# Rotary embedding and attention scores: TensorE's steps as a loop, its waits relayed by GpSimd, and the small rests of five loads moved to one queue

## The chip, the cores and the metric

The kernel runs on one core of one Trainium2 chip. The metric is the device time of one execution in microseconds (us). Lower is better. The runs of the kernel before took 791.87, 792.61 and 793.0 us; their median is 792.61.

## What is computed

```python
# q, k: (16, 512, 16, 64) float32 as batch, sequence, heads, dim; cos, sin: (512, 32)
q1, q2 = q[..., :32], q[..., 32:]
q_rot = concat(q1 * cos - q2 * sin, q1 * sin + q2 * cos)   # k_rot from k in the same way
scores = einsum('bshd,bthd->bsht', q_rot, k_rot)            # (16, 512, 16, 512) float32
```

The output has 268.4 MB and the two inputs have 67.1 MB, so for each 4 MB of scores that go out, 1 MB of inputs comes in.

## The kernel before

A sequence of 512 rows is cut into 4 slots of 128 rows (row 4p+c lies in partition p of slot c). One **step** `i` makes the scores of one slot of queries against all 512 keys of its batch `i // 4`: 16 heads in 8 pairs `p`, 64 steps in all. Steps 0 to 3 are batch 0; there the work is cut by heads, so that it can begin before the whole batch is loaded.

In `scores` (L194 to L217) each pair is two matmuls of 64 rows by 512 columns into one of three PSUM tiles `ps`; ScalarE (ACT) copies the tile to a staging buffer `st` of 4 MB (L212); after pair 7 SyncE (SP) issues the store of the whole buffer (L192). There are three such buffers, so step `i` can begin its copies when the store of step `i-3` has landed.

Beside that, each step prepares a later slot of q and one of k. `rope` (L128 to L163) is three VectorE (DVE) instructions on 1024 elements for each slot: the product with the sines goes to `part` (L153), the product with the cosines stays in place (L154), and so does the sum (L158). `transposed` (L165 to L189) turns four blocks of 128x128 by TensorE (PE) into a PSUM `bank`, and a copy takes them to `qT` or `kT` (L189), by DVE for q and by ACT for k. q is turned one step ahead, k four steps ahead; both `qT` and `kT` have two buffers. In steps from 4 on q is turned after pairs 1 and 3, k after pairs 5 and 6 (L269 to L297). The order of the instructions on each engine is the order of the code (`manual_schedule`, L227); the waits between engines are put in by the framework. Each engine waits for the others' semaphores itself.

`load` (L117 to L126) brings 2 MB of q or k, one batch, at the end of every second step of four: q after step 4m+2, k after step 4m+3. SP issues them in line with the stores. Five of them, named in `RELIEVED` (L77), go another way, `load_around` (L89 to L114): GpSimd (POOL) issues 120 of the 128 partitions as one DMA. The trace's packets show it on 15 of the 16 DMA engines, and one and the same engine is left out each time. The code chooses that engine by a cursor that it moves round the DMA engines: `move_cursor` (L82 to L87) pushes it on by a tiny DMA on `n` partitions. The last 8 partitions, the rest, are 64 pieces of 2 KB. For two of the loads (k of batches 7 and 12) POOL issues them, and their packets are on eight DMA engines, those that the code counts as 8 to 15; for the three others (q of batches 6, 11 and 15) ACT issues them, and their packets are on the other eight, 0 to 7.

Of the kernel before, what the change touches and what calls it, by code (L numbers as in the profile page):

```python
# [7 lines left out]

@with_exitstack  # L10
def kernel(
# [19 lines left out]
    G = H // C  # L31

    const_pool = ctx.enter_context(tc.tile_pool(name="const", bufs=1))
    in_pool = ctx.enter_context(tc.tile_pool(name="in", bufs=2))
    part_pool = ctx.enter_context(tc.tile_pool(name="part", bufs=1))
    kt_pool = ctx.enter_context(tc.tile_pool(name="kt", bufs=2))
    qt_pool = ctx.enter_context(tc.tile_pool(name="qt", bufs=2))
    stage_pool = ctx.enter_context(tc.tile_pool(name="stage", bufs=3))
    ps_s_pool = ctx.enter_context(tc.psum_pool(name="ps_s", bufs=3))
    ps_t_pool = ctx.enter_context(tc.psum_pool(name="ps_t", bufs=2))  # L40

# [11 lines left out]
    ss_v = ss_t.rearrange("p c x j -> p c (x j)")  # L53

    st_first = [stage_pool.tile([P, H, S], fp32, tag="stage", name="st") for _ in range(2)]
    early = stage_pool.tile([P, 2 * C * H * D], fp32, tag="stage", name="early")
    units = {}
    used = [0]  # L60

    def load_units(which, head, heads, queues):
        n = C * heads * D
        t = early[:, used[0] : used[0] + n].rearrange("p (c e) -> p c e", c=C)
        used[0] += n
        src = dram[which][0, :, :, head : head + heads, :]
        dst = t.rearrange("p c (h d) -> p c h d", d=D)
        m = C // len(queues)
        for x, queue in enumerate(queues):
            queue.dma_start(dst[:, m * x : m * (x + 1)], src[:, m * x : m * (x + 1)])  # L70
        for h in range(0, heads, G):
            units[which, (head + h) // G] = t[:, :, D * h : D * (h + G)]

    batches = {}

# [3 lines left out]
    scratch = const_pool.tile([P, 96], fp32, name="scratch")  # L79
    tiny = [0]  # L80

    def move_cursor(n):  # L82

        y = tiny[0]
        tiny[0] += 1
        src = bass.AP(q.tensor, 512 * y, [(512, n), (64, 2), (1, 2)])
        nc.gpsimd.dma_start(scratch[:n, 4 * y : 4 * y + 4].rearrange("p (a b) -> p a b", a=2), src)  # L87

    def load_around(which, b, t):  # L89

        n, E, SMALL = 120, C * H * D, C * H * D // 8
# [3 lines left out]
        def pieces(queue, lo, hi, F):  # L97
            k = E // F
            src = bass.AP(d.tensor, d.offset + lo * E + E - F, [(E, hi - lo), (-F, k), (1, F)])
            v = t[lo:hi].rearrange("p c e -> p (c e)")  # L100
            dst = bass.AP(v.tensor, v.offset + E - F, [v.ap[0], (-F, k), (1, F)])
            queue.dma_start(dst, src)  # L102

        if x == 0:
            nc.gpsimd.inc_swdge_sem([], [], mode="reset_dge_cursor")
        else:

            move_cursor(16 - SLOW)
        if x % 2:
            move_cursor(8)  # L110
            pieces(nc.gpsimd, n, P, SMALL)
        move_cursor(SLOW + 1)
        pieces(nc.gpsimd, 0, n, E // 2)
        if not x % 2:  # L114
            pieces(nc.scalar, n, P, SMALL)

    def load(which, b):  # L117

        if b >= B:
            return  # L120
        t = in_pool.tile([P, C, H * D], fp32, tag=which + "_in", name=which + "_sb")
        batches[which, b] = t
        if (which, b) in RELIEVED:
            load_around(which, b, t)
        else:
            nc.sync.dma_start(t.rearrange("p c (h d) -> p c h d", h=H), dram[which][b])  # L126

    def rope(which, n):  # L128

        part = part_pool.tile([P, H * D], fp32, tag="part", name="part")
        if n < C:
            x = units[which, n]
            sv, k1, k2 = "p c (g j) -> p c g j", {"j": HD}, {"j": D}
            cs = cos_t.unsqueeze(2).to_broadcast((P, C, 2 * G, HD))
            ss = ss_v.unsqueeze(2).to_broadcast((P, C, G, D))
            pv = part.rearrange("p (c g j) -> p c g j", c=C, j=D)
            x5 = x.rearrange("p c (h x j) -> p c h x j", x=2, j=HD)
            p5 = part.rearrange("p (c h x j) -> p c h x j", c=C, x=2, j=HD)
            adds = [(x5[:, :, :, y], p5[:, :, :, 1 - y]) for y in range(2)]  # L140
        else:
            x = batches[which, n // C][:, n % C]
            sv, k1, k2 = "p (g j) -> p g j", {"j": HD}, {"j": D}
            cs = cos_t[:, n % C].unsqueeze(1).to_broadcast((P, 2 * H, HD))
            ss = ss_v[:, n % C].unsqueeze(1).to_broadcast((P, H, D))
            pv = part.rearrange(sv, **k2)
            x4 = x.rearrange("p (h x j) -> p h x j", x=2, j=HD)
            swapped = bass.AP(part.tensor, part.offset + HD, [part.ap[0], (D, H), (-HD, 2), (1, HD)])
            adds = [(x4, swapped)]
        xs, xc = x.rearrange(sv, **k2), x.rearrange(sv, **k1)  # L150

        def products():
            nc.vector.tensor_tensor(pv, xs, ss, op=mult)  # L153
            nc.vector.tensor_tensor(xc, xc, cs, op=mult)  # L154

        def sums():
            for y, z in adds:
                nc.vector.tensor_tensor(y, y, z, op=add)  # L158
# [3 lines left out]
    kT = {}  # L162
    qT = {}  # L163

    def transposed(which, n, g, copy):  # L165

        bank = ps_t_pool.tile([P, 4, P], fp32, tag="ps_t", name="bank")
        for x in range(4):
            if n < C:  # L170
                src = units[which, n][:, x, P * g : P * (g + 1)]
            else:
                src = batches[which, n // C][:, n % C, P * (4 * g + x) : P * (4 * g + x + 1)]
            nc.tensor.transpose(bank[:, x, :], src, ident)  # L174
        src = bank
        if which == "q":
            if n not in qT:
                qT[n] = qt_pool.tile([P, HP, P], fp32, tag="qT", name="qT_t")
            dst = qT[n][:, 4 * g : 4 * g + 4, :]
        else:  # L180
            b = n // C
            if b not in kT:
                kT[b] = kt_pool.tile([P, HP, S], fp32, tag="kT", name="kT_t")
            if n < C:
                dst = kT[b][:, 2 * n + g].rearrange("p (t c) -> p t c", c=C)
                src = bank.rearrange("p c t -> p t c")
            else:
                dst = kT[b][:, 4 * g : 4 * g + 4, P * (n % C) : P * (n % C + 1)]
        copy(out=dst, in_=src)  # L189

    def store(i, st):
        nc.sync.dma_start(o_v[i // C, i % C], st)  # L192

    def scores(i, p, st):  # L194

        ps = ps_s_pool.tile([P, 2, S], fp32, tag="ps_s", name="ps")
        b = i // C
        if b == 0:
            c, hp = divmod(p, 2)
            lhs, rhs = qT[i][:, C * hp + c], kT[0][:, 2 * i + hp]  # L200
        else:
            lhs, rhs = qT[i][:, p], kT[b][:, p]
        for r in range(2):
            po, rh = ps[:, r, :], rhs[64 * r : 64 * r + 64, :]
            nc.tensor.matmul(  # L205
                out=po, lhsT=lhs[64 * r : 64 * r + 64, :], rhs=rh, start=True, stop=True
            )
# [4 lines left out]
        nc.scalar.copy(out=so, in_=si)  # L212
        if b == 0 and p % 2 == 1:
            c = p // 2
            nc.sync.dma_start(o_v[0, c, :, G * i : G * (i + 1)], st[:, G * c : G * (c + 1)])
        elif b > 0 and p == HP - 1:
            store(i, st)  # L217

    def tr_act(which, n):
        for g in range(2):  # L220
            transposed(which, n, g, nc.scalar.copy)
# [5 lines left out]
    with tc.manual_schedule():  # L227
        nc.scalar.dma_start(sin_t, sin.rearrange("(p c) j -> p c j", c=C))
        load_units("k", 0, G, (nc.sync, nc.scalar))
        nc.sync.dma_start(cos_t, cos.rearrange("(p c) j -> p c j", c=C))  # L230
        load_units("q", 0, G, (nc.sync, nc.scalar))
        load_units("k", G, H - G, (nc.sync,))
        load_units("q", G, H - G, (nc.sync,))
        load("k", 1)
        load("q", 1)
        make_identity(nc, ident)
        nc.scalar.copy(out=ss_t[:, :, 0, :], in_=sin_t)
        nc.scalar.mul(ss_t[:, :, 1, :], sin_t, -1.0)
        for which in ("k", "q"):
            run(rope(which, 0))  # L240
            tr_act(which, 0)

        for i in range(C):
            st = st_first[i] if i < 2 else stage_pool.tile([P, H, S], fp32, tag="stage", name="st")
            if i < C - 1:
                dve = rope("k", i + 1) + rope("q", i + 1) + rope("k", C + i)
                nxt = [("k", i + 1), ("q", i + 1)]
            else:
                dve = rope("q", C) + rope("k", C + i) + rope("q", C + 1) + rope("k", 2 * C)  # L250
                nxt = [("q", C), ("k", C + i)]
            for p in range(HP):
                scores(i, p, st)
# [72 lines left out]
```

## Time and profile before

| What | us |
|---|---|
| Median of three runs (791.87 to 793.0) | 792.61 |
| Span of the profiled execution, first to last instruction | 789.9 |
| The median of the runs stands above that span by | 2.7 |
| End of the last DMA packet, in the span | 788.6 |
| PE busy (matmuls), DVE busy, ACT busy | 687.7, 543.8, 561.2 |
| Mean duration of one copy of a pair by ACT (L212, 512 of them) | 1.020 |
| Mean duration of one rope instruction by DVE (L153, L154, L158) | 1.22 |
| Store of 4 MB, median from issue to landing | 25.2 |

The span is the profiled execution's time without what lies around it (the launch and the end of the program); the page gives no other time of that execution. The view of busy time tells how long each engine worked, not whether anybody waited for it. That is told by the view of waits and by the slices of DMA: there a digit is the share of time, in tenths, in which the 16 DMA engines had a packet in work. Packets are the pieces that a DMA engine moves; the trace holds each one's queue, start, duration and size.

### The profile page before, as it was taken

The page shows a single profiled execution, that of the slowest core. Times are in us where ns is not written, and L with a number is a line of the kernel's source. Part 1 is how long each engine was busy: PE and PEld are TensorE (multiplying, and loading weights), DVE is VectorE, ACT ScalarE, POOL GpSimd, SP SyncE. Part 2 cuts the span into 40 slices and gives each one's busy share as a digit, 9 for nine tenths or more (in the row PEclk, how much of TensorE's full clock was granted, in tenths as well). Part 3 has the DMA queues.
Part 4 walks back from the last instruction along what each step waited for, and adds up shares of the span by engine and source line. Part 5 has one row for each costly group of instructions (what it writes and reads, how often), then busy time and mean ns, then how long its engine had stood idle before and what let it go on. Part 6 is the DMA issues. An engine that isn't in the chain of part 4 may idle for free.

```text
span 789.9 us, 7753 instructions
## 1 busy us (share of the span) xinstructions
PE 687.7 (87%) x3072; PEld 297.4 (38%) x3072; DVE 543.8 (69%) x516; ACT 561.2 (71%) x647; POOL 11.9 (2%) x24
## 2 busy tenths in 40 slices
PE   4999998989978989798897988989899798899960
PEld 2444443433423434243343433434334343344420
DVE  7999987667855859566676666767678486587400
ACT  3888886866847868486685865877577586588770
POOL 0000000000001000000000000100000000000000
PEclk9999999999998999899899898999899899899995
DMA  9999999999999999999999999999999999999997
GB/s 353 421 426 440 429 431 435 424 434 440 428 427 429 429 425 406 428 431 436 430 431 434 427 431 427 429 432 429 427 437 422 437 433 433 428 431 436 430 431 339
DMA packets 19100, 336.18 MB, mean 426 GB/s; under 512 B 2376, under 2 KB 3656, under 8 KB 4936
## 3 DMA queue, kind: packets, MB, share of 16 engines
q1 hardware_dynamic: 16288, 324.61, 96.1%
q0 software_dynamic: 1872, 10.10, 3.1%
q10 hardware_dynamic: 904, 0.98, 0.4%
q8 instruction: 24, 0.39, 0.2%
q14 instruction: 12, 0.10, 0.0%
HBM read 67.24 MB, written 268.44 MB: 425 GB/s over the span
## 4 chain that ended last, share of the span: by engine, by line
DMA 46%; PE 39%; DVE 7%; ACT 4%; issue 1%; ACTq 0%
DMA out_dram<-st 45%; PE ps L205 29%; PE bank L174 9%; ACT st L212 4%; DVE part L153 2%; DVE early L154 1%; DVE early L158 1%; DMA early<-in_q_dram 1%; DVE k_sb L158 1%; DVE k_sb L154 1%; DVE kT_t L189 0%; DVE q_sb L154 0%; DVE q_sb L158 0%; ACTq L321 0%; DVE qT_t L189 0%
## 5 line engine op out<-in xcount | busy, mean ns | idle before, releaser
L212 ACT COPY st<-ps 128x1024 f32<-128x1024 f32 x512 | 495.0, 1020 | 193.7 <-DMA out_dram<-st 109.1
L205 PE MATMUL ps<-kT_t,qT_t 64*128 64x512 f32 x2048 | 545.6, 650 | 64.3 <-ACT st L212 64.1
L205 PEld LDWEIGHTS ps<-kT_t,qT_t 64*128 64x128 f32 x2048 | 183.3, 196 | 255.3 <-issue 135.4
L189 DVE COPY qT_t<-bank 128x512 f32<-128x512 f32 x118 | 81.5, 690 | 186.5 <-PE bank L174 186.5
L174 PEld LDWEIGHTS bank<-ident,q_sb 128*128 128x128 f32 x480 | 55.4, 151 | 100.5 <-issue 97.6
L174 PE MATMUL bank<-ident,q_sb 128*128 128x128 f32 x480 | 86.8, 308 | 0.4 <-PE ps L205 0.4
L174 PEld LDWEIGHTS bank<-ident,k_sb 128*128 128x128 f32 x480 | 50.3, 140 | 94.6 <-issue 42.3
L174 PE MATMUL bank<-ident,k_sb 128*128 128x128 f32 x480 | 78.6, 287 | 1.2 <-DVE qT_t L189 1.2
L153 DVE TENSOR_TENSOR part<-k_sb,ss_t 128x1024 f32<-128x1024 f32 x60 | 72.9, 1215 | 9.3 <-DMA k_sb<-in_k_dram 9.2
L189 ACT COPY kT_t<-bank 128x512 f32<-128x512 f32 x122 | 72.4, 598 | 6.9 <-PE bank L174 6.9
L154 DVE TENSOR_TENSOR k_sb<-k_sb,cos_t 128x1024 f32<-128x1024 f32 x60 | 73.5, 1225 | 2.0
L158 DVE TENSOR_TENSOR k_sb<-k_sb,part 128x1024 f32<-128x1024 f32 x60 | 73.5, 1225 | 2.1
L154 DVE TENSOR_TENSOR q_sb<-q_sb,cos_t 128x1024 f32<-128x1024 f32 x60 | 73.5, 1225 | 2.1
L153 DVE TENSOR_TENSOR part<-q_sb,ss_t 128x1024 f32<-128x1024 f32 x60 | 73.5, 1224 | 2.0
L158 DVE TENSOR_TENSOR q_sb<-q_sb,part 128x1024 f32<-128x1024 f32 x60 | 72.9, 1215 | 0.0
L174 PE MATMUL bank<-ident,early 128*128 128x128 f32 x64 | 10.5, 316 | 12.2 <-DVE early L158 9.7
L174 PEld LDWEIGHTS bank<-ident,early 128*128 128x128 f32 x64 | 8.3, 161 | 17.3 <-issue 13.9
L153 DVE TENSOR_TENSOR part<-early,ss_t 128x1024 f32<-128x1024 f32 x8 | 9.8, 1222 | 5.7 <-DMA early<-in_k_dram 4.9
L102 POOL DMA_DIRECT2D q_sb<-in_q_dram x3 | 2.3, 754 | 617.4 <-PE bank L174 617.4
L158 DVE TENSOR_TENSOR early<-early,part 128x512 f32<-128x512 f32 x16 | 10.3, 685 | 0.2
L154 DVE TENSOR_TENSOR early<-early,cos_t 128x1024 f32<-128x1024 f32 x8 | 9.8, 1225 | 0.3
L189 ACT COPY qT_t<-bank 128x512 f32<-128x512 f32 x10 | 5.7, 628 | 3.3 <-PE bank L174 3.3
(12 smaller groups left out, 15.9 us busy)
## 6 DMA issues: line engine op xcount, KB each, us to landing
out_dram<-st SPq DMA_DIRECT2D x60, 4096.0 KB, 25.2
k_sb<-in_k_dram SPq DMA_DIRECT2D x13, 2048.0 KB, 27.7
q_sb<-in_q_dram SPq DMA_DIRECT2D x12, 2048.0 KB, 27.6
out_dram<-st SPq DMA_DIRECT2D x16, 1024.0 KB, 14.5
q_sb<-in_q_dram POOLq DMA_DIRECT2D x3, 1920.0 KB, 29.2
k_sb<-in_k_dram POOLq DMA_DIRECT2D x2, 1920.0 KB, 43.2
early<-in_k_dram SPq DMA_DIRECT2D x1, 1536.0 KB
early<-in_q_dram SPq DMA_DIRECT2D x1, 1536.0 KB, 12.4
```

Of the source, the lines that this page charges most:

```text
L102: queue.dma_start(dst, src)
L153: nc.vector.tensor_tensor(pv, xs, ss, op=mult)
L154: nc.vector.tensor_tensor(xc, xc, cs, op=mult)
L158: nc.vector.tensor_tensor(y, y, z, op=add)
L174: nc.tensor.transpose(bank[:, x, :], src, ident)
L189: copy(out=dst, in_=src)
L205: nc.tensor.matmul(out=po, lhsT=lhs[64 * r : 64 * r + 64, :], rhs=rh, start=True, stop=True)
L212: nc.scalar.copy(out=so, in_=si)
```

## The change

The whole order of work and all semaphores are now written by the kernel itself. A class `Plan` records for each operation what it reads and writes, and makes the waits from that. Then:

- **The loop.** PE's instructions for steps 4 to 59 are written once for two steps and run 28 times. So that an instruction can be the same in each turn, the buffers stand still: one `qT`, one `kT`, and one `kN` into which the next batch's k is turned; DVE copies `kN` to `kT` in two halves at the last step of a batch (`next_kT`, after pairs 3 and 7).
- **The relay.** PE waits for one counter per phase only. For each group of PE instructions POOL waits for what the group needs and then raises that counter by one. At the end of a step PE waits for the full count and takes it off again.
- **The order in a step.** k is now turned after pairs 1 and 2 (copied by ACT), q after pairs 4 and 7 (copied by DVE). DVE's k sines follow pair 2, k cosines and sums pair 4, and all three q operations pair 7.
- **rope** of a slot writes its result to `turned`, one buffer for q and one for k, instead of in place; PE reads it there. So a load waits for DVE's rope, no longer for PE's transposes. The score tiles and banks are named by pair and half.
- **The loads.** All five loads of `load_around` now have their rest issued by POOL, ahead of the 120 partitions, and ACT issues none. SP's loads and stores stand in the same order as before.

The built program has, for POOL, 838 instructions in place of 76 (774 of them semaphore instructions), and for PE 320 matmul instructions in place of 2048. The core of the diff:

```diff
+    def op(self, engine, emit, reads=(), writes=()):
+        needs = self._needs(reads, writes)
+        if engine == PE:
+            waits = self._waits(POOL, needs, skip=(PE,))
+            lane, n = self.phase, self.relays.get(self.phase, 0) + 1
+            self.relays[lane] = n
+            self.ops[POOL].append(("relay", waits, lane))
...
+            self.ops[PE].append(("group", (lane, n), emit))
+        else:
+            self.ops[engine].append(("op", self._waits(engine, needs), emit))
+        self._done(engine, 1, engine, reads, writes)
...
-        if x % 2:
-            move_cursor(8)
-            pieces(nc.gpsimd, n, P, SMALL)
+        move_cursor(8)
+        pieces(f"w{which}{b % 2}r", n, P, small)
         move_cursor(SLOW + 1)
-        pieces(nc.gpsimd, 0, n, E // 2)
-        if not x % 2:
-            pieces(nc.scalar, n, P, SMALL)
+        pieces(f"w{which}{b % 2}m", 0, n, E // 2)
...
+    for i in range(C, NST):
+        if C <= i < LAST:
+            plan.enter(f"turn{(i - C) % UNROLL}")
+        elif i == LAST:
+            plan.enter("end")
+        last = i % C == C - 1 and i + 1 < NST
+        k_ops = rope_slot("k", i + 1 + C) if i + 1 + C < NST else []
+        q_ops = rope_slot("q", i + 2) if i + 2 < NST else []
+        for p in range(HP):
+            scores(i, p)
+            if p in (1, 2) and i + C < NST:
+                transposed("k", i + C, p - 1, ACT)
+            if p == 2:
+                run(k_ops[:1])
+            if p == 3 and last:
+                next_kT(0)
+            if p == 4 and i + 1 < NST:
+                transposed("q", i + 1, 0, DVE)
+                run(k_ops[1:])
+            if p == 7 and last:
+                next_kT(1)
+            if p == 7 and i + 1 < NST:
+                transposed("q", i + 1, 1, DVE)
+        run(q_ops)
+        if i % C == C - 2:
+            load("q", i // C + 2)
+        elif i % C == C - 1:
+            load("k", i // C + 3)
...
+            if kind == "relay":
+                for s, v in waits[:-1]:
+                    eng.wait_ge(sem(s), v)
+                if waits:
+                    eng.wait_ge(sem(waits[-1][0]), waits[-1][1]).then_inc(sem(fn), 1)
+                else:
+                    eng.sem_inc(sem(fn), 1)
+                continue
...
+        nc.tensor.addr_align(256)
+        with nc.tensor.Fori(0, (len(turns) - 1) // UNROLL):
+            for x in range(UNROLL):
+                mine = ops[turns[x] + 1 : turns[x + 1]]
+                for o in mine:
+                    emit_group(*o[1:])
+                lane = sem(f"turn{x}")
+                nc.tensor.wait_ge(lane, len(mine)).then_inc(lane, -len(mine))
```

`addr_align(256)` puts the loop's first instruction at a multiple of 256 instructions.

## The prediction

> **What bounds it now.** I read the slices of the page first, then the DMA queues, then the stretches around the start and the end.
>
> ```profile
> span 789.9 us, 7753 instructions
> PE 687.7 (87%) x3072; PEld 297.4 (38%) x3072; DVE 543.8 (69%) x516; ACT 561.2 (71%) x647; POOL 11.9 (2%) x24
> DMA  9999999999999999999999999999999999999997
> q1 hardware_dynamic: 16288, 324.61, 96.1%
> q0 software_dynamic: 1872, 10.10, 3.1%
> q8 instruction: 24, 0.39, 0.2%
> q14 instruction: 12, 0.10, 0.0%
> ```
>
> No slice but the last has an idle tenth of DMA, while no compute engine reaches 90%. The bound is DMA work. It falls with packets that go away, or with a better spread of them, since the last of the 16 DMA engines sets the end. Two stretches, one in the first full steps and one at the end, tell how much cover compute has (after the width come PE, PEld, DVE, ACT, POOL, then granted clock, DMA share, GB/s):
>
> ```profile
> 73.50:83.50 10.00, 10.00 (x50) 4.43 (x48) 9.83 (x10) 8.67 (x11) 0.00 (x0) 1.00 1.06 456
> 780.00:789.00 9.00, 0.00 (x0) 0.00 (x0) 0.00 (x0) 0.00 (x0) 0.00 (x0) 0.50 0.63 273
> ```
>
> In the first PE has no gap: a step takes PE 10.02 us (stores are issued at 73.2, 83.2 and 93.2). By packet records a 4 MB store gives each DMA engine 8 packets of 1,213 ns, 9.70 us, and a 2 MB load 8 of 611 ns, 4.89 us. Four steps carry 4 stores and 2 loads, 48.6 us, 12.15 a step, so compute has 2.1 us to spare per step. In the second stretch compute is done and DMA at 63%: the engines end at different times.
>
> **The 16 ends.** A packet that starts where another ended, within some ns, is on the same DMA engine. Followed so from 20 us on, the records fall into 16 chains. They end between 782.3 and 788.6 us, mean 786.0. What sets them apart is the instruction fetch. The 24 packets of q8 (16,384 B for 256 instructions: 0.39 MB over PE's 6,144) lie on eight chains, 2 to 4 on each, and these end at 786.3 to 788.6. Of the five chains with no fetch, four end at 782.3, 782.5, 783.2 and 783.3 (the fifth, 785.4, had long packets near 300 us). A fetch takes 0.88 to 1.05 us and the packet behind it 0.4 more, 1.3 us in all. The q14 packets (8,192 B) lie on three chains: six on one, at 125 to 150 us spacing as ACT's some 740 instructions need, four (788.5) and two (788.6). That last chain is the one that POOL's loads leave out; most of its store packets take 1,227 to 1,270 ns instead of 1,213. I call it the slow engine.
>
> **The change, part by part.**
>
> *Loop.* PE's stream shrinks to about 960 instructions (96 a step by the page, 10 steps written out): 4 or 5 fetches instead of 24. The six chains of 8 to 15 with fetches drop to 782.4, or 783.7 with one left; the two of 0 to 7 to 783.3. Taken from the mean of all engines that is 20 x 1.3 / 16 = 1.6 us.
>
> *Rests.* Engines 0 to 7 lose three rests of 8 packets of 84 ns each: 2.0 us. Engines 8 to 15 gain three of 4 packets of 163 ns (the form that POOL's rests have now): 2.0 us.
>
> *POOL's instructions.* 838 instead of 76: at 128 per 8,192 B some 6 fetches, of 0.31 us plus 0.12 (ACT's) to 0.35 (DVE's) on the packet behind, 2.6 to 4.0 us on one chain that the trace can't name.
>
> *Sum of ends.* 8 to 15: 782.4 + 2.0 = 784.4, with a fetch 785.7. 0 to 7 without fetches: 781.3. The chain with four q14 packets: 788.5 - 2.0 = 786.5; the slow engine: 788.6 - 2.0 = 786.6. POOL's fetches: 784 to 785 on 0 to 7, 787 to 788 on 8 to 15. I take 786.6: **-2.0 us**.
>
> *Start and end.* The kernel is now a block of its own, with a handshake ahead of it and one behind. The meeting of the engines at the start (L310, 0.54 to 0.69) and at the end (L321, 789.16 to 789.39) takes 0.15 to 0.23 us; one more at each side: **+0.2 to +0.5**, I take 0.3.
>
> *Relays.* 12 groups a step each pass one more hop; the meeting above shows 0.08 us between POOL's semaphore instructions and about as much to the others. Unhidden: 12 x 0.1 = 1.2 us a step, 11.2 against 12.15. Below, nothing: PE is behind its conditions, not waiting for them, in stretches where it sets the pace. I take nothing, since the queue of stores covers it. The cover is thinnest where no loads come: issued less moved bytes show 4.5 to 4.7 us of DMA work in queue when steps 4 to 6 issue their stores, and about 7 in steps 56 to 59.
>
> *Loop entry.* The padding ahead of the loop (at most 255 instructions, here some 40) has no row; the nearest, semaphore instructions 0.04 to 0.08 us apart, gives 0 to 3 us once. It falls where PE must wait anyway: step 4 turns k after pair 1, at about 63.3, but DVE ends that slot's rope at 65.50. That moves the stores of step 4 by 1.0 us, and at 0.3 a step steps 5 and 6 by 1.6: 4.5 - 1.6 leaves 2.9. Nothing.
>
> *kN to kT.* Two DVE copies of 2048 elements each fourth step. DVE's row for 512 elements from PSUM is 0.69 us, so 2.2 us each, 4.4 per four steps; DVE works 6 x 1.22 + 2 x 0.69 = 8.7 a step, so 9.8 of 12.15. Hidden.
>
> Net: -2.0 + 0.3 = -1.7, span 788.2. The runs' median stands 2.7 above the profiled span; with that unchanged, 790.9 us.
>
> **Rivals.**
>
> *(a) Late k loads empty the queue: slower.* POOL's packets alternate with SP's on each engine, so each takes a turn of 1.2 us. The k loads already come late:
>
> ```profile
> q_sb<-in_q_dram POOLq DMA_DIRECT2D x3, 1920.0 KB, 29.2
> k_sb<-in_k_dram POOLq DMA_DIRECT2D x2, 1920.0 KB, 43.2
> ...
> DVE part L153 <- DMA k_sb<-in_k_dram: 9.2, 2, 4.6
> ```
>
> k of batch 7 is issued at 250.4 while q of 6 is still moving (until 257). Between the two loads of 120 partitions stand the tiny DMAs and the rest: 11 turns, 12.8 us, then 24.7 for the load itself, landing at 293.05; DVE waits 4.6 us. Now q has its own tiny DMAs and rest ahead (9 turns, 10.4 us, for batch 6; 12.8 for 11), and POOL comes to it some 4 us later, behind the step's relays (the step's store is issued at 234.2, q of 6 now at 228). q of 6 then lands near 268 and k of 7 near 268 + 37.5 = 305; k of 12 near 553 instead of 538. DVE stands before its sines and behind it wait the copies of kT and qT that the next step's first matmuls need. From landing to that step's store I count 18 us: sines 1.2, kN copy 2.2, qT copy 0.7, the q rope behind until 13.4, then three pairs and the last copy. The queue that is there runs until 305.5 + 17.1 + 3 (the part of k not yet moved) = 325.5; the store comes at 323. For 12 it is 571 against 571. So the point from which it decides is a landing 2 us later than I count for k of 7, and just my count for k of 12. Each us beyond costs 1, less some 2 us by which the engines that end last are behind the mean. Price 2 to 4 us at each: 793 to 799.
>
> [...]
>
> *(b) The gain goes to another engine: no change.* POOL's fetches land on one of 8 to 15 (787 to 788), or the slow engine catches up less than it did; or PE fetches the loop's block again at each turn. [...] All give 792 to 793.
>
> The trace has no loop. [...]
>
> *(c) PE becomes the bound: slower.* If relays and branch add over 2.1 us to each step, each 0.1 beyond costs 56 x 0.1 = 5.6 us. That needs 0.18 us unhidden at all 12 groups. 795 to 810.
>
> **Chances.** Forecast, ends balanced and queue never empty: 0.53, 790.9, by itself 789 to 792. (a) 0.22. (b) 0.17. (c) 0.05. A larger gain (no chain above 785) 0.03, faster. A measurement of this kernel can tell about 0.2%, 1.6 us, from no change: below 791.0 is faster, above 794.2 slower. The forecast lies at that bound; of it I count 0.42 as faster and 0.11 as same; (a) 0.17 slower, 0.05 same; (b) 0.15 same, 0.02 slower; (c) slower. Faster 0.45, same 0.31, slower 0.24. The range begins at perfect balance (all chains at the mean, 786.0 - 1.6 = 784.4, with 0.2 of start and end: 788.6) and leaves out the upper half of (a) and most of (c): 788.6 to 796.0.
>
> **What would show it.** Right: q8 with 4 to 6 packets, DMA still at 9 in all slices but the last, POOL's queue with rests in place of ACT's, chains ending closer together near 786.6, PE's idle before L333 put to POOL without the stores being late. (a): a wait of 12 us or more of DVE on a k load, and a slice of DMA below 9 or a lower GB/s just behind it, near 325 and 571. (b): q8 still at 20 packets or more, or one chain far behind. (c): PE busy near 95% with idle DMA in every slice. I am wrong if DMA is idle in steps 4 to 10, or if the slow engine ends after 789.

## The result, and the profile after

The change made the kernel slower: 812.22 us (median of four runs, 811.75 to 813.26) against 792.24 (four runs, 791.84 to 793.0) on the same chip, a ratio of 1.0246 with a 95% interval of 1.0231 to 1.0261. The forecast was 790.9, the range ended at 796.0. The profiled execution spans 811.5 us instead of 789.9.

From the page of the changed kernel, the lines that answer to those of before (queue lines: packets, MB, share of 16 engines):

```profile
span 811.5 us, 8761 instructions
PE 673.8 (83%) x3072; PEld 292.3 (36%) x3072; DVE 572.3 (71%) x544; ACT 554.4 (68%) x647; POOL 16.9 (2%) x30
...
DMA  8998599999999999999999999999999999999996
GB/s 343 425 426 367 233 410 412 431 430 430 424 437 431 426 424 400 435 433 416 434 433 435 426 434 432 411 426 414 422 417 388 435 426 434 428 435 430 432 430 302
...
q0 software_dynamic: 2208, 10.49, 3.2%
...
q14 instruction: 18, 0.15, 0.0%
q8 instruction: 4, 0.07, 0.0%
```

The fetches did go, 24 packets to 4, and POOL's came, 12 to 18. But the DMA line has a hole in its fifth slice (81 to 101 us), where 233 GB/s were moved, and shallower dents in the GB/s at the 16th (400, 304 to 325 us) and the 31st (388, 609 to 629); the kernel before has a dent of 406 in its own 16th slice, but 422 in its 31st. The stretches around the hole (columns as in the prediction: after the width PE, PEld, DVE, ACT, POOL, then granted clock, DMA share, GB/s):

```profile
58.00:62.00 4.00, 4.00 (x22) 1.73 (x18) 3.93 (x4) 4.00 (x6) 0.00 (x0) 1.00 1.02 422
62.00:77.00 15.00, 0.15 (x2) 0.00 (x0) 4.12 (x4) 1.21 (x2) 0.00 (x0) 0.66 1.02 432
77.00:79.00 2.00, 1.89 (x6) 0.94 (x8) 0.00 (x0) 0.00 (x0) 0.00 (x0) 0.50 0.57 238
79.00:81.00 2.00, 2.00 (x9) 0.63 (x6) 0.00 (x0) 1.21 (x2) 0.00 (x0) 0.62 0.02 8
```

PE does nothing for 15 us, from 62 to 77; DMA lives on its queue until 78 and then stops. The view of waits says who waited for what (engine, line, tile, releaser: us in all, times, longest):

```profile
ACT st L278 <- PE ps L333: 115.7, 96, 21.5
...
DVE kr L224 <- DMA k_sb<-in_k_dram: 44.9, 2, 22.5
...
DVE kr L224 <- PE bank L290: 16.8, 1, 16.8
PE ps L333 <- issue: 15.0, 1, 15.0
```

DVE and ACT wait for PE, and PE's 15 us have as releaser "issue": it waited for nothing but its own instruction stream. The view of line 489, `addr_align(256)`, shows what that stream holds (shortest, median and longest ns, first and last start):

```profile
L489 PEldq NOP  x238: 13/13/13, 59.6 to 77.0; - x119
```

That is the padding ahead of the loop: 238 NOPs (instructions that do nothing), one each 0.073 us (17.4 us in all). The store of step 4 is issued at 89.8 us instead of 73.5. (Issue times from here on are the ends of the issuing instructions; the prediction's 73.2 is the start of the same one.)

The second line, two waits of 22.5 us for a k load, is rival (a):

```profile
q_sb<-in_q_dram POOLq DMA_DIRECT2D x3, 1920.0 KB, 38.1
k_sb<-in_k_dram POOLq DMA_DIRECT2D x2, 1920.0 KB, 57.5
```

From issue to landing q takes 38.1 us (29.2 before) and k 57.5 (43.2). The k loads of batches 7 and 12 land at 319.2 and 567.2; the next step's store then finds 3.3 and 0.5 us of DMA work in queue.

**Where the 21.6 us of span are.** Followed as in the prediction, the 16 chains end at 804.8 to 807.9, mean 805.8, where before they ended at 782.3 to 788.6, mean 786.2 by the same count. The mean can be taken apart by the packets. *Idle* is the time without a packet, mean of the 16 engines, from 10 to 780 us. *Excess* is what the load and store packets took beyond their usual durations (1,213 ns for 32 KB, 611 for 16 KB, 309 for 8 KB and so on), over 16 engines. Idle rose from 0.1 to 13.8, excess from 4.9 to 11.1, the idle time in the first 10 us by 0.5, and fetches fell by 1.1: 13.7 + 6.3 + 0.5 - 1.1 = 19.4 of the 19.6. The last engine is 2.0 behind the mean instead of 2.4, and from the last packet to the end of the span it takes 3.6 us instead of 1.3.

### The profile page after: what moved, and what is told of

It reads as the page before. It is cut to its first block, busy times and chain, and to the rows that moved or that the text cites. A ratio compares the mean times of both kernels' runs of the same rounds, so it can differ in the third digit from the quotient of the medians.

```text
span 811.5 us, 8761 instructions
## 1 busy us (share of the span) xinstructions
PE 673.8 (83%) x3072; PEld 292.3 (36%) x3072; DVE 572.3 (71%) x544; ACT 554.4 (68%) x647; POOL 16.9 (2%) x30
## 4 chain that ended last, share of the span: by engine, by line
PE 37%; DMA 37%; ACT 8%; DVE 8%; another core or an unknown queue 6%; issue 2%; ACTq 0%; POOLq 0%; DVEq 0%; SPq 0%
DMA out_dram<-st 36%; PE ps L333 29%; PE bank L290 8%; ACT st L278 8%; DVE qr L224 2%; DVE st L224 2%; DVE kr L224 1%; DVE kT L276 1%; DVE q_sb L224 1%; DVE k_sb L224 1%; DMA st<-in_k_dram 0%; ACT kN L278 0%; DVE qT L276 0%; ACTq L161 0%
## 5 line engine op out<-in xcount | busy, mean ns | idle before, releaser
L333 PE MATMUL ps<-kT,qT 64*128 64x512 f32 x1920 | 500.6, 641 | 97.6 <-POOLq L465 81.4
L333 PEld LDWEIGHTS ps<-kT,qT 64*128 64x128 f32 x1920 | 169.3, 193 | 271.3 <-POOLq L465 161.9
L276 DVE COPY qT<-bank 128x512 f32<-128x512 f32 x118 | 81.5, 690 | 100.8 <-PE bank L290 100.6
L224 DVE TENSOR_TENSOR kr<-k_sb,ss_t 128x1024 f32<-128x1024 f32 x60 | 73.1, 1219 | 61.9 <-DMA k_sb<-in_k_dram 44.9
L290 PE MATMUL bank<-ident,qr 128*128 128x128 f32 x480 | 81.9, 295 | 1.4 <-POOLq L465 1.2
L290 PE MATMUL bank<-ident,kr 128*128 128x128 f32 x480 | 79.1, 288 | 0.3 <-POOLq L465 0.3
L278 ACT COPY kN<-bank 128x512 f32<-128x512 f32 x120 | 72.4, 605 | 6.8 <-PE bank L290 6.8
L224 DVE TENSOR_TENSOR kr<-k_sb,kr 128x1024 f32<-128x1024 f32 x60 | 73.5, 1225 | 2.0
L224 DVE TENSOR_TENSOR q_sb<-q_sb,cos_t 128x1024 f32<-128x1024 f32 x60 | 73.5, 1225 | 2.0
L224 DVE TENSOR_TENSOR qr<-q_sb,qr 128x1024 f32<-128x1024 f32 x60 | 73.5, 1225 | 2.0
L224 DVE TENSOR_TENSOR qr<-q_sb,ss_t 128x1024 f32<-128x1024 f32 x60 | 72.9, 1215 | 0.0
L276 DVE COPY kT<-kN 128x2048 f32<-128x2048 f32 x28 | 34.3, 1224 | 28.8 <-PE ps L333 20.4
L290 PEld LDWEIGHTS bank<-ident,st 128*128 128x128 f32 x64 | 8.3, 161 | 17.4 <-POOLq L465 16.6
## 6 DMA issues: line engine op xcount, KB each, us to landing
out_dram<-st SPq DMA_DIRECT2D x16, 1024.0 KB, 13.8
q_sb<-in_q_dram POOLq DMA_DIRECT2D x3, 1920.0 KB, 38.1
k_sb<-in_k_dram POOLq DMA_DIRECT2D x2, 1920.0 KB, 57.5
```

The lines of the kernel that those rows point to most:

```text
L224: plan.op(DVE, lambda: nc.vector.tensor_tensor(out_ap, a, b, op=op), reads, writes)
L276: plan.op(DVE, lambda: nc.vector.tensor_copy(out=dst, in_=src), reads, writes)
L278: plan.op(ACT, lambda: nc.scalar.copy(out=dst, in_=src), reads, writes)
L290: return [nc.tensor.transpose(bank[:, x, :], srcs[x], ident) for x in range(4)]
L333: nc.tensor.matmul(out=ps[:, r, :], lhsT=lhs[64 * r : 64 * r + 64, :], rhs=rhs[64 * r : 64 * r + 64, :], start=True, stop=True,)
```

## The experiments

Theory P: the padding ahead of the loop. Rival K: the late k loads. Rival R: relays and loop lengthen each step. The last columns are from the profiled execution: idle and excess as above, then the mean and the last end of the 16 chains.

| Kernel | Median, us | Ratio to before, 95% | Idle | Excess | Mean end | Last end |
|---|---|---|---|---|---|---|
| before | 792.2 to 792.7 | 1 | 0.1 | 4.9 | 786.2 | 788.6 |
| after | 812.22 | 1.0231 to 1.0261 | 13.8 | 11.1 | 805.8 | 807.9 |
| e1 padding branched over | 801.36 | 1.0076 to 1.0139 | 2.6 | 9.4 | 793.0 | 795.1 |
| e2 q rests by ACT | 811.08 | 1.0213 to 1.0247 | 12.8 | 8.3 | 801.4 | 806.4 |
| e3 both | 797.26 | 1.0043 to 1.0085 | 0.1 | 5.8 | 786.6 | 791.4 |
| e5 written out | 800.57 | 1.0081 to 1.0115 | 2.5 | 10.1 | 794.6 | 797.0 |
| e4 before, rests moved | 793.90 | 1.0009 to 1.0026 | 0.1 | 6.4 | 787.8 | 791.9 |
| e6 e1, early loads | 798.37 | 1.0044 to 1.0083 | 0.7 | 8.8 | 790.3 | 794.2 |
| e7 e6, early drain | 796.76 | 1.0040 to 1.0074 | 0.2 | 6.8 | 787.6 | 791.3 |
| e10 e7, q rests by ACT | 795.56 | 1.0023 to 1.0046 | 0.1 | 6.1 | 786.7 | 791.7 |
| e11 no loop, no relays | 797.05 | 1.0040 to 1.0066 | 0.1 | 7.4 | 789.1 | 793.1 |
| e13 e10, k slot first | 794.59 | 1.0013 to 1.0031 | 0.1 | 4.2 | 785.0 | 790.6 |
| e14 e7, k slot first | 795.44 | 1.0021 to 1.0045 | 0.2 | 7.3 | 788.1 | 792.2 |
| e15 e13 without loop, relays, early loads | 793.28 | 1.0000 to 1.0018 | 0.1 | 4.7 | 786.4 | 789.5 |

### The padding: e1, e9, e8

```diff
-        nc.tensor.addr_align(256)
+        nc.tensor.addr_align(256, max_nops=0)
```

With `max_nops=0` the padding is branched over instead of executed.

> The changed kernel with the padding ahead of the loop branched over instead of executed (at most one instruction of it runs). Theory P (the 238 padding instructions hold TensorE for 17 us, and the DMA engines idle 12.4 us of it): 812.2 - 12.4 = 799.8, or 794 if the 6 us by which packets took longer in the changed kernel also come from engines that run in step after the idle stretch. Theory K (the late k loads, landing at 319 and 567, are what costs): 810 to 812. Theory R (relays and loop make each step longer): 812. The profile: TensorE idle ahead of the loop goes from 15.0 us to under 3, the store of step 4 is issued near 74 instead of 89.8.

801.36: 10.9 us less than after; the mean end fell by 12.8. In the same stretch of e1 where PE stood still:

```profile
62.00:77.00 15.00, 12.85 (x63) 5.45 (x61) 10.82 (x11) 11.36 (x14) 0.00 (x0) 1.00 1.02 430
```

The store of step 4 is issued at 74.4. P holds for the most of it. R falls as the cause of the most of it: whatever the loop and the relays cost is in e1 too. But 9 us are left.

e9 executes fewer pads, by placing the loop at slot 128 of a block; e8 has the same place with the pads branched over.

```diff
-        nc.tensor.addr_align(256)
+        nc.tensor.addr_align(256, offset=128)
```

> The same placement with the padding executed: 110 padding instructions instead of 238. At 0.0715 us each from 59.57 us they end near 67.4 us; the relay that the loop's first matmul waits for came at 66.3. Padding that costs only beyond that relay: store of step 4 near 75.5 us, no idle DMA, the time of the same kernel without padding within 1.5 us. Padding that costs for each instruction: 7.9 us more DMA idle and time.

> Padding branched over, but the loop begins in the middle of a fetch block (slot 128 of 256), so its some 200 instructions lie over two blocks. If the loop stays resident when it lies over two blocks: q8 at 4 to 6 packets and the time of the kernel with the padding branched over, 798 to 803. If a block is fetched again at each of the 28 turns: q8 at 30 to 60 packets, 1.3 us each over 16 engines: 2 to 5 us more, and TensorE idle at each turn.

e9: 806.43 us (one run), 110 pads (128 fewer than in after), store of step 4 at 81.5 and not 75.5: my threshold was wrong. I had taken the relay of 66.3 for the one that the first matmul waited for; e8 shows PE at work on step 4 from 62.7. So pads count from about 62. e9's stretches (clock in the third column from the end):

```profile
62.00:67.60 5.60, 0.07 (x2) 0.00 (x0) 4.06 (x4) 1.13 (x2) 0.00 (x0) 0.92 1.02 429
67.60:69.00 1.40, 1.29 (x4) 0.84 (x6) 0.00 (x0) 0.00 (x0) 0.00 (x0) 0.50 1.01 427
69.00:71.00 2.00, 2.00 (x6) 0.43 (x4) 0.00 (x0) 1.01 (x1) 0.00 (x0) 0.50 1.01 426
71.00:73.00 2.00, 2.00 (x8) 1.23 (x8) 0.00 (x0) 1.43 (x2) 0.00 (x0) 0.50 1.04 438
```

PE stands for 5.6 us, and comes back at a granted clock of 0.50 for some 6 us more. From the traces: the first matmul of step 4 is 5.0 us later than in e8 (67.7 against 62.7); the wait for k of 1.9 us that e8 has in step 4 is gone; the slow clock takes the rest, about 3.5, of the 6.7 us by which the store is later (81.5 against 74.8). The queue held 3.9 us when e8 issued that store; past it DMA stands idle (5.9 us against 1.8). So pads are neither free up to a relay nor 0.073 us each: they cost what they hold PE beyond 62 us, plus the clock, less the queue, and then what the emptied queue costs. That last part is not small: 6.7 less 3.9 is 2.8 us, but at the stores of steps 4 to 6 the queue holds 0.0, 0.7 and 0.7 us, and from 60 to 120 us e9 has 4.2 us of idle and 1.9 of excess more than e8, 6.1 of the 6.2 us by which its mean end is later (799.1 against 792.9).

e8: 799.36 us (one run), within the runs of e1, and its page has the same line as after:

```profile
q8 instruction: 4, 0.07, 0.0%
```

The body of some 200 instructions over two blocks was not fetched again in its 28 turns: 4 packets in all. The alignment was not needed for that.

### The late k loads: e2, e3, e4, e6

e2 issues the q rests by ACT, as before; e3 is e1 and e2 together.

```diff
-        move_cursor(8)
-        pieces(f"w{which}{b % 2}r", n, P, small)
+        if x % 2:
+            move_cursor(8)
+            pieces(POOL, f"w{which}{b % 2}r", n, P, small)
...
+        if not x % 2:
+            pieces(ACT, f"w{which}{b % 2}r", n, P, small)
```

> The changed kernel with the rests of the three q loads issued by ScalarE behind the main load again, as in the kernel before; padding still executed. P: 811 to 813, the padding is untouched. K: k of batch 7 lands near 300 instead of 319 and k of 12 near 548 instead of 567, DVE waits for k fall from 44.9 us to under 20, and the time falls by 2 to 8 us, to 804 to 810.

> Both edits: padding branched over, q rests issued by ScalarE. P alone: as the kernel with the padding branched over, within 1 us. K on top of P: 2 to 8 us below that one. If nothing else was wrong with the loop, the span is that of the kernel before (789.9) less some 1.6 us of fetches, plus 2.6 us of start and end: 790 to 792, a time of 793 to 795.

With the padding in, moving the rests back brings only 1.1 us (811.08, as P had it); with it out, 4.1 (797.26). In e2 the landing times fall by 8.3 us for k of 7 and 7.2 for k of 12 against after, where K had expected 19, and DVE's two waits for k by 14.7 (30.2 instead of 44.9), where K had expected 25 or more. So K has the direction; its size with the padding in is a miss. In e3 k of 7 lands at 297.9 instead of e1's 305.0. The stretches behind the two landings, of e1 and then of e3:

```profile
320.00:360.00 40.00, 40.00 (x194) 17.69 (x192) 35.95 (x35) 34.69 (x41) 0.00 (x0) 1.00 0.99 409
560.00:610.00 50.00, 50.00 (x238) 21.80 (x234) 45.42 (x43) 42.77 (x50) 0.00 (x0) 0.98 0.96 396
```

```profile
320.00:360.00 40.00, 39.86 (x194) 17.41 (x192) 36.02 (x34) 33.15 (x40) 0.00 (x0) 1.00 1.01 432
560.00:610.00 50.00, 50.00 (x242) 22.11 (x240) 44.39 (x43) 42.79 (x51) 0.00 (x0) 1.00 1.00 431
```

In both PE is busy all the time: it sets the pace here, a step in 10.02 us. What differs is the queue. With stores issued into 0.3 to 1.9 us of queued work (e1) the DMA share is 0.96 to 0.99, but the rate is 5 to 8% lower: idle time and longer packets come together. Idle and excess make 6.1 us of the mean (2.6 + 9.4 against 0.1 + 5.8). K holds; the evidence is the difference between e1 and e3. The ranges of their runs overlap by 0.6 us (798.0 to 802.7 and 795.7 to 798.6), so the packets are the stronger evidence.

e4 makes the same move alone, in the kernel before.

```diff
-        if x % 2:
-            move_cursor(8)
-            pieces(nc.gpsimd, n, P, SMALL)
+        move_cursor(8)
+        pieces(nc.gpsimd, n, P, SMALL)
...
-        if not x % 2:
-            pieces(nc.scalar, n, P, SMALL)
```

> The kernel before with one edit: the three q rests go by GpSimd ahead of the main load, as in the changed kernel; TensorE unrolled, no relays. If moving the rests only evens out the engines: the chains of 0 to 7 fall by 2.0 us and those of 8 to 15 rise by 2.0, and as the latter still carry their fetches the last one ends near 790 instead of 788.6: 793 to 794. Theory K: q of batch 6 lands near 267 instead of 257 and k of 7 near 303 instead of 293, k of 12 near 548, DVE's waits for k rise from 9.2 us to 25 to 30, and the packets' excess rises by 1 to 3 us: 794 to 797. If the rests by GpSimd gain by themselves: 790 to 791.

793.90, 1.35 us above before. Its DVE waits:

```profile
DVE part L150 <- DMA k_sb<-in_k_dram: 27.0, 2, 15.0
```

The wait came, but k of 7 lands at 301.0 and the queue still holds 9.8 us at that step's store. In the profiled execution, the slowest of the eleven runs (795.15), the mean end is 1.6 us later, nearly all of it excess (6.4 against 4.9), and the last engine is 4.2 behind the mean instead of 2.4. So the loss is longer packets and spread in about equal parts. By the chains' packets, those with 12 packets of POOL's rests from 310 us on and one or two fetches of PE end at 788.9 to 791.9, those with neither at 784.2 to 784.5. Without the loop the rests are put on the very engines, 8 to 15, that carry most of PE's fetches (six of the eight chains with fetches in before).

e6 leaves the rests with POOL, and lets POOL issue its loads inside the step.

```diff
+            if p == 2 and i % C == C - 1 and ("k", i // C + 3) in RELIEVED:
+                load("k", i // C + 3)
...
+                if i % C == C - 2 and ("q", i // C + 2) in RELIEVED:
+                    load("q", i // C + 2)
```

> Padding branched over, all rests by GpSimd as in the changed kernel, but GpSimd's five loads issued inside the step instead of at its end (q behind the first q transposes of the step, k behind its second k transposes), some 5 us earlier for q and 9 for k. Theory K (a k load that lands late empties the queue): k of batch 7 lands near 300 instead of 305 and k of 12 near 549 instead of 554; the idle of the DMA engines at 320 to 360 and 560 to 610 (2.6 us on the mean with the padding branched over) goes to nearly nothing, the packets' excess falls by 2 to 4 us: 793 to 796. If the GpSimd rests cost by themselves (their packets, their turns), the time stays at 800 to 802.

798.37, 3.0 us below e1 (the ranges of the runs overlap); idle fell by 1.9. But k of 7 lands at 303.1, not 300 (305.0 in e1): issuing k 10 us sooner brings 1.9. In before the packets of POOL's two loads follow one another: the last 8 KB packet of q of 6 ends at 256.2, and the rest of k of 7, issued at 249.1, begins at 259.1. That k waits behind q in e6 too is my reading.

### Loop and relays: e5, e11

e5 writes all steps out, and keeps the relays. e11 lets PE wait for its conditions itself too.

```diff
-        nc.tensor.addr_align(256)
-        with nc.tensor.Fori(0, (len(turns) - 1) // UNROLL):
+        for turn in range((len(turns) - 1) // UNROLL):
```

```diff
-            waits = self._waits(POOL, needs, skip=(PE,))
...
+            self.ops[PE].append(("group", self._waits(PE, needs, skip=(PE,)), emit))
```

> The changed kernel with TensorE's steps written out: no loop and no padding, the relays by GpSimd and GpSimd's loads as they are. P: as the kernel with the padding branched over, plus 1.6 us for 20 more fetches (q8 back near 24 packets): 795 to 802. If the loop itself (branch, refetch) cost anything, this kernel is below that one. R (relays): still near 812.

> The changed kernel's order of work with TensorE written out and waiting for its conditions itself: no loop, no padding, no relays by GpSimd, loads and rests as in the changed kernel. To be held against the same with relays (800.57). Theory R (a relay costs TensorE something at each group): stores closer than 10.02 us apart in stretches where TensorE sets the pace, and 5 us or more less. Relays that cost nothing there but hold up GpSimd's load instructions: stores still 10.02 us apart, q of batch 6 issued near 228 instead of 232, k of 7 landing some 4 us earlier, 1 to 3 us less. No effect at all: 800.

e5: 800.57, not to be told from e1 by these runs (their ranges overlap), but the mean end is 1.63 us later than e1's and its page has 24 fetches again:

```profile
q8 instruction: 24, 0.39, 0.2%
```

So the loop is worth about 1.6 us of mean DMA time, as counted: 1.2 are the fetches' own packets, the rest is excess, and e5's slower clock in step 4 (below) has some 0.3 of that. PE loses nothing to the loop that shows. e11: 797.05, 3.5 below e5. Where PE sets the pace its stores are 10.02 us apart in both (e5: 322.55, 332.57, 342.58), so a relay costs PE nothing that shows there. It holds up POOL: q of batch 6 is issued at 223 us without relays and 233 with them, k of 7 lands at 294.7 instead of 306.0, and idle falls from 2.5 to 0.1. The relays' price is paid through K.

### The end: e7

```diff
         nc.gpsimd.wait_ge(sem("tiny"), plan.count["tiny"])
+        nc.gpsimd.drain()
```

> As the kernel with earlier loads, with one more drain as GpSimd's last instruction inside the block, behind its last relay. If GpSimd's drain of 2.02 us at the end of the block is the cost of retiring its software transfers, it runs beside the last stores now and the second one takes 0.1 us: 1.9 us below the kernel with earlier loads. If it is the handshake itself, no change.

796.76 against 798.37; the medians' difference is within their spread, but the trace shows it: POOL's drain at the end of the block takes 0.04 us instead of 2.02, and the last packet stands 1.8 us ahead of the span's end instead of 3.6. In after that drain was 2.02 us too, on the path that sets the end. Before, POOL drained from 667.9 to 697.3 us, beside the stores.

### What was left: e10, e12, e13, e14, e15, e16

e10 takes together what helped: e6, e7 and the q rests by ACT. e12 also moves DVE's k operations behind the first q copy (`run(k_ops[:1])` after pair 2 goes, `run(k_ops)` after pair 4).

> The loop kept, padding branched over, q rests on ScalarE again, GpSimd's loads issued inside the step, GpSimd drained early. Theory K says that with both the queue is never empty: no idle DMA between 10 and 780 us, excess near the 4.9 us of the kernel before, mean end 1 us below that of before (786.2) by the fetches, the last engine at 789 to 790, time 792 to 794. If it stays at 796 to 797 like the kernel with early loads and early drain, the late k loads were not what is left.

> As the kernel with early loads, rests on ScalarE and early drain, with DVE's k rope moved as a whole behind the step's first q copy, so that a k load that is not there yet no longer holds up that copy. If DVE's wait for k still costs: 1 to 2 us less, 791 to 793. If the queue was never empty any more: the same within 0.5 us.

795.56 and 795.94 (e12's ratio: 1.0020 to 1.0045). Hardly any idle DMA, and still 3 us above before. DVE's wait for k fell from 21.6 us in e10 to 13.3 in e12 with no gain in time: what is left of it costs nothing that these runs show. The times of e10 range from 793.1 to 798.0. Its first stretches of step 4:

```profile
64.00:66.00 2.00, 0.49 (x3) 0.50 (x4) 1.37 (x2) 0.70 (x1) 0.00 (x0) 0.80 1.01 418
66.00:68.00 2.00, 2.00 (x7) 0.72 (x6) 0.00 (x0) 0.59 (x1) 0.00 (x0) 0.50 1.03 434
```

PE waits 1.87 us for the k that it turns after pair 1 (DVE's rope ends at 65.4), and then the clock is at 0.50. The store of step 4 is issued at 76.0, and the excess from 100 to 120 us is 1.28. The profiled executions of e5, e6, e11 and e12 show the same clock and stores at 75.9 to 77.5; those of e1, e3, e7 and e8 have the gap of 1.86 us too, but the clock at 1.00 and stores at 74.2 to 74.8. The later the store, the thinner the queue, and the excess from 100 to 120 us goes with it: with 3.3 us or more in queue at the store of step 6 it is at most 0.08 (e1, e3, e4, e7, e8 and before), with 2.6 it is 0.40 (e5), with 1.9 it is 1.28 (e10), with 1.7 it is 1.51 (e11), with 1.3 it is 1.55 (e12), with 1.0 it is 1.85 (e6). e13 exchanges two lines ahead of the loop.

```diff
-    run(rope_slot("q", C + 1))
     run(rope_slot("k", 2 * C))
+    run(rope_slot("q", C + 1))
```

> As the kernel with early loads, rests on ScalarE and early drain (795.56), with DVE's two ropes ahead of the loop exchanged, the k slot of batch 2 first. Theory G (TensorE's gap of 1.87 us at the first k transposes of step 4, behind which the granted clock falls to 0.50 for some 3 us in part of the executions, thins the queue to 2.6 us and brings 1.3 us of packet excess at 100 to 120): the k slot is ready 3.7 us earlier, no gap, clock 1.00, store of step 4 near 72.5, queue near 6 us, excess at 100 to 120 under 0.1, time 792.5 to 794. If the gap has nothing to do with the rest: 795 to 796.

> The same with all rests by GpSimd as in the changed kernel. Theory G: 1 to 3 us below the kernel with early loads and early drain (796.76). Against the one with the rests on ScalarE: its k loads land some 7 us later, the engines end closer together; 0 to 2 us above it.

e13: 794.59, runs from 793.8 to 794.9, excess 4.2, the store at 74.3 (not 72.5). In its profile:

```profile
64.00:66.00 2.00, 1.47 (x10) 0.62 (x8) 2.00 (x2) 1.60 (x3) 0.00 (x0) 1.00 1.02 426
66.00:68.00 2.00, 2.00 (x12) 0.84 (x12) 1.93 (x3) 1.52 (x3) 0.00 (x0) 1.00 1.00 418
```

The gap took 1 us and most of the scatter. e14, with the rests by POOL, is 1.3 below e7 and 0.85 above e13.

e15 has e13's order, rests and drain, with PE written out and waiting for itself, and POOL's loads at the end of the step as in the change.

> TensorE written out, waiting for itself, no relays, rests on ScalarE, k slot first, early drain: what of the kernel's new order of work is left without loop and relays. q8 at 24 packets; GpSimd's loads issued 8 us earlier than with relays; k never late. If the loop's fetches are worth their 1.3 us net of the relays, it ends 1 us above the looped kernel with the k slot first; if the relays' hold on GpSimd costs more than the fetches save, below it.

793.28: 1.3 below e13, though its mean end is 1.3 above it. By the chains, e13's ends spread over 8.6 us: the slow engine is last (790.6) and three chains with 3 or 4 fetches of ACT or POOL from 320 us on are at 786.9 to 789.2; the other twelve are at 782.0 to 784.4, but for two (787.2 and 788.5). The slow engine ends at 786.8 in e15, with the same loads; from 320 us on its stores took 1,253 ns on the mean in e15, 1,260 before, 1,263 in e13, 1,271 in e8. I found no reason for these differences, and where two packets end within some ns of each other a chain can be followed wrongly, so the slow engine's figures are less certain than the 16 ends.

e16 takes work off the engines that end last in e13: one more load goes round the slow engine, and the rest of q of batch 15 goes by POOL instead of ACT. The lines for the first:

```diff
-    RELIEVED = {("q", 6): 0, ("k", 7): 1, ("q", 11): 2, ("k", 12): 3, ("q", 15): 4}
+    RELIEVED = {("q", 6): 0, ("k", 7): 1, ("k", 9): 2, ("q", 11): 3, ("k", 12): 4, ("q", 15): 5}
```

> As the kernel with the k slot first and the rests on ScalarE (794.59; its 16 engines end at 781.9 to 790.6, mean 785.0, the slow engine last), with one more load that leaves the slow engine out (k of batch 9, by GpSimd) and the rest of q of batch 15 by GpSimd. If the spread of the ends is all that still separates it from the kernel before: the slow engine ends 4.5 us earlier, the last one is a chain with ScalarE's or GpSimd's fetches near 788.9, 1.7 us earlier: 792 to 793.5. If the load of batch 9 by GpSimd comes late or adds packet excess: 794 to 797.

796.67, a miss. The spread shrank (787.4 to 792.6), but the excess rose from 4.2 to 9.1, of it 4.7 between 340 and 380 us, while that load was moved (issued 333.2, landed 370.7). So this load by POOL costs more in other packets' time than it takes off the slow engine. No version here beats the kernel before; e15 comes nearest (ratio 1.0000 to 1.0018).

## Why the prediction was wrong

- **Loop entry** is the step that failed: "at most 255 instructions, here some 40", "0 to 3 us once", "Nothing". There were 238 pads. PE's own instructions ahead of the loop are 464 (232 matmuls, 232 weight loads, by the trace), as I had counted; but 238 pads mean that they would have ended at slot 18 of a block, 66 slots further on. So there are instructions that the trace doesn't show, or the stream doesn't begin at a boundary; the runs don't tell which. The price per pad (0.04 to 0.08) was right. I put my own count where the text itself gave 255 as the bound: 255 x 0.08 = 20 us stood in reach of a queue of 4.5, and neither rival nor range took it in. What the runs showed in place of "Nothing": PE stands for 15.0 us, the queue of 4.5 us runs out, and DMA is idle during step 4. Idle DMA in steps 4 to 10 was a sign of being wrong that the prediction itself had named. Price: 10.9 us by e1, 13.8 by e2 against e3.
- **Rival (a)** came true as well, with the times that it named: k of 7 at 305.0 and k of 12 at 554.5 in e1, for 305 and 553. Its price, 2 to 4 us each, was about right at its lower end: 4.1 in all by e3. It should have been part of the forecast at 0.22: my own count had the queue and the store level to the microsecond at 571.
- **Relays.** Right for PE (10.02 us a step before and after), wrong as "nothing": they hold up POOL's loads. The delay was as I said against before (q of batch 6: the rest, now ahead, issued at 231.8 in e1 and the load itself at 233.2; the load at 228.5 before), but 10 us against the same order without relays, and that is worth 3.5 us by e11. I had put it into (a) and not into the sum.
- **Loop.** Right in the mean: 4 fetches, 1.63 us of mean end between e5 and e1. No run shows it in the time: e1 is not below e5, and e13, with 4 fetches, is 1.3 above e15, with 24 (which differs in the relays and in the place of POOL's loads too). **POOL's instructions.** Right: 6 fetches more. The loop's block was not fetched again: 4 packets of q8 in after and in e1, 4 with the body over two blocks (e8). So a fetch at each turn, the last case of (b), and what PE would wait for it, no run shows.
- **Rests.** The 2.0 us did move, but not the end. In after the ends lie within 3.0 us; that looks like the balance that I forecast, and is not: with POOL's rests and hardly any idle DMA the ends lie within 5.8 (e7) and 6.2 us (e14), with the q rests by ACT and all else the same within 7.5 (e10) and 8.6 (e13). So the move itself is worth some 2 us of spread, and yet e7 and e14 take 1.2 and 0.85 us longer than e10 and e13: their mean ends are later, with more excess. I take the rest of the 3.0 for the empty queue, at which the early engines wait for the late ones; that is argued, not shown.
- **Sum of ends.** 786.6 was not reached by any version. The sum rests on "What sets them apart is the instruction fetch", and for PE's fetches that did not hold: before, with 24 of them, the ends lie within 6.3 us, and with 4 and hardly any idle DMA within 7.3 (e3), 7.5 (e10) and 8.6 (e13). The mean of e13, 785.0, is where the loop's gain is seen; the slow engine, which I had at 786.6, ended between 786.8 and 792.2 without idle DMA.
- **Start and end.** 0.3 us was 0.5 at the start and 2.3 at the end: the block's exit drains POOL, 2.02 us, which the meeting of engines in the trace of before could not show, as POOL had drained there earlier.
- **kN to kT.** 1,224 ns for 2048 elements (28 copies in after), not the 2.2 us that I had estimated from the row of 512 elements out of PSUM. For (a) I had counted 18 us from landing to the store, with 2.2 for a kN copy; in e1 it took 16.5 (554.5 to 570.9), about 1.5 less. But k of 12 landed 1.5 us later than counted, so the store stood at 571 all the same.
- **(c)** fell: PE busy 83%. The time would not have been in the range even without the padding: e1 is 801.36.

## What to carry to other kernels

Instructions that do nothing took time here, 0.073 us each (238 in 17.4 us): ask for what an alignment costs at its bound, and whether the loop needs it at all. When an engine is given a second job (passing on waits), look at what its own queue was for; the relays cost the engine that they serve nothing that showed (10.02 us a step with and without them), and delayed the loads of the one that runs them (by 10 us for q of batch 6). In a kernel bound by DMA read the depth of the queue of stores at each store: here it was the cover for every small delay (4.5 us at the store of step 4), and a thin queue lost twice, by idle engines and by longer packets (13.8 and 11.1 us in after, 0.1 and 4.9 before). A smaller spread of ends need not be balance: 3.0 us in after, 6.3 before.

## What the runs showed of the hardware

- A NOP of the padding took 0.073 us on PE's sequencer (after), and that ran ahead of the matmuls: the pads began at 59.57, while PE's matmuls ran until 62.1.
- After 5.6 us without matmuls (e9) the granted clock was 0.50 for some 6 us. With a gap of 1.86 to 1.91 us it fell to 0.50 for 3.4 us in five profiled executions (e5, e6, e10, e11, e12) and stayed at 1.00 in four (e1, e3, e7, e8); with gaps of up to 1.23 us (before, e4) it stayed at 1.00. What decides between them the runs don't show.
- POOL's first drain after its DMAs took 2.02 us with 24 such DMAs (after, e1, e7) and 1.53 with 18 (e3, e10, e13), with all of them long landed; a second one took 0.04.
- Behind stores issued into less than 2 us of queued work the engines moved 396 to 409 GB/s (e1) instead of 431 to 432 (e3), in packets that took longer (9.4 us of excess instead of 5.8), not only in gaps (2.6 us of idle instead of 0.1). Why the packets took longer stays open.
- The cursor shows in the packets of before. Ahead of k of batch 7 the tiny DMAs on 12 and 8 partitions put 20 packets of 16 bytes on the 16 chains: one on each of the eight that carry the rest and on four others, two on each of the last four, of which one is the slow engine. The tiny DMA on 5 partitions has one on each of the four others and one on the slow engine, and the load behind it is on all but the slow engine.
